# A hybrid encoder layer: keys and first queries summed while the normalised input comes in quarters, attention ahead of the late rows' queries, and a gate in column tiles

## The chip, the cores and the metric

The kernel runs on one core of a Trainium2 chip. The metric is the device time of one execution in microseconds (us), as the median of several runs. The core has five engines with an instruction queue each: TensorE (PE), VectorE (DVE), ScalarE (ACT), GpSimd (POOL) and SyncE (SP). Each engine executes its queue in order and waits on semaphores for the others. All transfers of this kernel are issued by SP.

## What is computed

One encoder layer is applied to two groups of 1024 rows of 1024 numbers ("prompt" and "sample"), which share the weights and have a conditioning vector c each. In short, for one group:

```python
mod = silu(c) @ w_ada + b_ada
shift, scale, gate = split(mod, 3)
h = rms_norm(x, norm_g) * (1 + scale) + shift
qa, ka, va, za, qb, kb, vb, zb, ga, gb = split(h @ w_in)     # 5376 columns in all
# branch A: 8 query heads, 2 key and value heads, 64 wide
oa = attention(rope(norm(qa)), rope(norm(ka)), va) * silu(za)
# branch B: 4 heads with two softmax maps each, values 128 wide
pd = softmax(q0 k0) - lam * softmax(q1 k1)
ob = rms_norm(pd @ vb, subln_g) * (1 - lam_init) * silu(zb)
merged = sigmoid(ga) * (oa @ w_proj_a) + sigmoid(gb) * (ob @ w_proj_b)
y = x + gate * (merged @ w_out)
```

## The kernel before

The numbers are 32-bit floats. Most products are made from a rounded high part and a remainder of each operand (`h` has parts `hh` and `hl`, a weight `w` has two parts in one tile): three matmuls for each block of 128 inputs, hh x w-high, hh x w-low and hl x w-high. ACT makes the high part by a copy, DVE the remainder by a subtraction.

The transposed input lies as eight blocks of 128 channels by 1024 rows, in two halves of 512 rows. Every piece of work is a generator that yields after each portion of TensorE work, and `weave` (line 71) interleaves generators by how far each has come relative to its planned number of portions; tables of numbers at the top (lines 37 to 60) set these plans for each group and phase. A scheduler then orders the instructions on each engine, so the order on an engine is not simply that of the code.

- `start` (line 337) loads w_ada's parts for shift and scale (eight tiles of 512 x 512), the first half of x, the weight for keys and values, and the second half of x. `ada` (line 292) multiplies c with w_ada, TensorE giving two output rows of 512 columns at a time (line 298). `inv_rms` and `spread` make 1/rms of each row from squares (line 254), and `modulated` makes h's parts for the first half of the rows, `start_late` for the second.
- `kva_gen` and `qa_gen` sum keys with values, and queries, tile by tile of 128 rows (`proj_tt`, line 515: 24 matmuls with 256 columns). A front part normalises and rotates on ACT, DVE and POOL, a back part transposes (line 568). Before attention starts, the head has summed eight tiles of keys and eight of the first queries.
- `z_gen` sums a gate path: four units a call of 24 matmuls with 512 columns (line 704), 48 units in a group. They are the filler: `Z_HEAD` and `Z_SHARE` say how many run in which phase.
- `attention` (line 872) makes for each tile of 128 queries four score matmuls (lines 737 and 738; the second takes a copy of the queries with halves swapped by a transfer), a maximum on DVE (739), an exponential on ACT (741), a transpose on DVE (774) and a transfer that completes it, then the products with the values (799 and 800 in branch A, 839 in branch B). There are 64 score tiles in branch A and 64 in branch B in a group; they are counted through here, 0 to 127 for the first group and 128 to 255 for the second.
- At the end of attention `gate_gen` multiplies c with the gate's third of w_ada (line 452, 16 matmuls, first group alone), and `gated_gen` multiplies the outputs by their gates; for branch B it puts 1/rms of each row into 128 equal rows by four transposes for each block and half (line 942). `merge_gen` (976) and `out_gen` (1007) do the last products; `TAIL` portions of branch A's merge are kept until attention is over.

PSUM has two large tiles for scores ("s"), three of one bank ("f") and one for values ("a"). Outside attention the "f" requests may take an "s" tile (`gbank`, line 120).

## Time and profile before

| | us |
|---|---|
| median of 3 runs | 1944.24 |
| lowest and highest run | 1936.62, 1945.65 |
| profiled execution | 1933.24 |
| its span, first to last instruction | 1931.5 |
| TensorE busy | 1881.2 |
| DVE busy | 1397.3 |
| ACT busy | 991.7 |
| POOL busy | 414.7 |

The profile is of one execution. A row of a group names the line of the kernel, the engine, the operation, output and input tiles without their numbers, shapes and count; then the busy time of the group, the mean duration of one instruction in ns, and how long the engine had idled before them with what ended most of that. A matmul of full 32-bit floats (line 298, for example) appears as two passes. A row of a stretch of time has the busy time of PE, PE's weight loads, DVE, ACT and POOL, each with its number of instructions, then the clock that TensorE was granted (1.00 is full speed), the busy share of the transfer engines and GB/s. Matmuls overlap, so the mean duration of one is longer than what it adds to the busy time.

### The profile page before, as it was taken

To read this page: it belongs to the slowest core of one execution; us is meant where nothing else is said; L and a number is where in the kernel's file an instruction comes from. 1 tells how busy PE (TensorE), PEld (TensorE's weight loads), DVE (VectorE), ACT (ScalarE), POOL (GpSimd) and SP (SyncE) were. 2 spreads that over 40 slices of the span, in tenths; PEclk is the share of its full clock that TensorE was granted. 3 is DMA by queue.
4 is the path that set the end of the run, shared out by engine and by line. 5 is a ranking of instruction groups with operands and counts; after the bars stand their busy time and mean duration, and the time that the engine had idled before them with its cause. 6 is when DMAs were issued, how large, how long until landed. Compare 5 with 4: busy or idle time off the path is not lost.

```text
span 1931.5 us, 30797 instructions
## 1 busy us (share of the span) xinstructions
PE 1881.2 (97%) x10466; PEld 1610.0 (83%) x10466; DVE 1397.3 (72%) x2145; ACT 991.7 (51%) x2091; POOL 414.7 (21%) x758
## 2 busy tenths in 40 slices
...
GB/s 319 45 81 146 135 173 148 153 148 176 152 142 110 116 92 192 273 256 181 218 140 39 137 144 166 145 172 151 154 129 162 107 113 100 143 234 264 180 104 77
DMA packets 271613, 295.25 MB, mean 153 GB/s; under 512 B 37857, under 2 KB 220257, under 8 KB 271457
## 3 DMA queue, kind: packets, MB, share of 16 engines
...
## 4 chain that ended last, share of the span: by engine, by line
PE 81%; DVE 7%; DMA 5%; issue 2%; ACT 2%; SPq 1%; POOL 1%; DVEq 0%; ACTq 0%; POOLq 0%
PE f L704 22%; PE f L515 19%; PE f L1007 5%; PE s L737 5%; PE a L839 5%; PE s L738 5%; PE f L976 4%; PE s L1007 4%; PE a L800 3%; PE a L799 3%; PE s L976 2%; DMA q<-p 2%; DVE m L739 2%; DVE p L774 1%; PE f L298 1%
## 5 line engine op out<-in xcount | busy, mean ns | idle before, releaser
L704 PE MATMUL f<-u,w 128*128 128x512 f32 x2232 | 574.2, 395 | 2.0 <-DVE ssB L863 1.5
L515 PE MATMUL f<-w,u 128*128 128x256 f32 x3456 | 487.5, 285 | 7.5 <-DVE u L571 3.7
L515 PEld LDWEIGHTS f<-w,u 128*128 128x128 f32 x3456 | 457.8, 190 | 29.0 <-DVE u L571 4.3
L704 PEld LDWEIGHTS f<-u,w 128*128 128x128 f32 x2232 | 404.2, 188 | 77.8 <-DVE ssB L863 1.8
L739 DVE TENSOR_REDUCE m<-s 128x1 f32<-128x1024 f32 x256 | 311.0, 1217 | 51.3 <-PE s L738 48.4
L774 DVE STREAM_TRANSPOSE p<-p 128x1024 f32<-128x1024 f32 x192 | 238.3, 1241 | 92.7 <-ACT p L741 89.3
L738 PE MATMUL s<-u,sw 128*128 128x512 f32 x512 | 203.8, 398 | 0.0
L788 DVE TENSOR_TENSOR q<-q,hi 128x512 fp32r<-128x512 f32 x256 | 171.5, 690 | 34.3 <-ACT hi L787 32.3
L787 ACT ACTIVATE hi<-q 128x512 fp32r<-128x512 f32 x256 | 153.6, 624 | 76.2 <-DMA q<-p 37.8
L741 ACT ACTIVATE p<-s,m,rsA 128x1024 f32<-128x1024 f32 x128 | 153.8, 1202 | 71.4 <-DMA q<-p 69.6
L178 ACT ACTIVATE w<-st 128x512 fp32r<-128x512 f32 x196 | 114.4, 625 | 99.2 <-DMA st<-in_w_in_dram 42.4
L741 ACT ACTIVATE p<-s,m,rsB 128x1024 f32<-128x1024 f32 x128 | 154.3, 1205 | 6.5 <-DMA q<-p 1.9
L179 DVE TENSOR_TENSOR w<-st,w 128x512 fp32r<-128x512 f32 x196 | 132.8, 706 | 34.2 <-ACT w L178 33.1
L658 POOL TENSOR_TENSOR row<-row,gB 128x96 f32<-128x96 f32 x64 | 33.8, 528 | 485.7 <-ACT row L529 474.1
L799 PE MATMUL a<-hi,u 128*128 128x256 f32 x512 | 132.2, 284 | 2.8 <-DMA q<-p 1.8
L800 PE MATMUL a<-q,u 128*128 128x256 f32 x512 | 129.3, 286 | 2.6 <-DVE q L788 2.6
L976 PE MATMUL f<-u,w 128*128 128x512 f32 x540 | 130.5, 393 | 1.3 <-DVE u L987 1.3
L839 PE MATMUL a<-q,u 128*128 128x256 f32 x512 | 127.1, 385 | 3.9 <-DVE oo L816 3.0
L976 PEld LDWEIGHTS f<-u,w 128*128 128x128 f32 x540 | 100.5, 188 | 23.0 <-DVE u L987 2.3
L839 PEld LDWEIGHTS a<-q,u 128*128 128x128 f32 x512 | 95.6, 193 | 20.0 <-DVE oo L816 3.6
L737 PE MATMUL s<-u 128*128 128x512 f32 x256 | 108.3, 424 | 3.3 <-ACT p L741 3.2
L737 PE MATMUL s<-u,u 128*128 128x512 f32 x256 | 102.4, 400 | 8.5 <-ACT p L741 3.1
(181 smaller groups left out, 2557.5 us busy)
## 6 DMA issues: line engine op xcount, KB each, us to landing
...
sw<-u SPq DMA_DIRECT2D x256, 64.0 KB, 2.1
...
```

Of the source, the lines that this page charges most:

```text
L515: nc.tensor.matmul(ps, lt[c][:, sl], w[:, c, wi, :], start=(k == 0), stop=(k == 23))
L704: nc.tensor.matmul(ps, w[:, c, wi, e * P : (e + 1) * P], rt[c], start=(k == 0), stop=(k == 23),)
L737: nc.tensor.matmul(s[:, sl], q, k[:, sl], start=True, stop=False)
L738: nc.tensor.matmul(s[:, sl], sw, k[:, sl], start=False, stop=True)
L739: nc.vector.tensor_reduce(out=m, in_=s, axis=AX.X, op=ALU.max, negate=True)
L741: nc.scalar.activation(pt.rearrange("p (j c a) -> p j c a", j=4, c=8), s.rearrange("p (c a j) -> p j c a", c=8, j=4), AF.Exp, scale=rs, bi ...
L774: nc.vector.transpose(pt, pt)
L799: nc.tensor.matmul(acc, lt, th[:, c, :], start=(k == 0), stop=False)
L800: nc.tensor.matmul(acc, lt, tl[:, c, :], start=False, stop=(k == 7))
L839: nc.tensor.matmul(acc, u["v"][:, k], pT[:, k], start=(k == 0), stop=(k == 7))
L976: nc.tensor.matmul(ps, w[:, c, wi, d * P : (d + 1) * P], o[:, oi, :], start=(k == 0), stop=(k == 11))
L1007: nc.tensor.matmul(ps, w[:, c, wi, e * P : (e + 1) * P], m[:, mi, :], start=(k == 0), stop=(k == 23))
```

## The change

- The start: w_ada comes as four quarters of 256 channels, each with shift and scale, and x's first half ahead of them all on SP's queue. The weight for the first 256 query columns is loaded at the start too, and a gate weight after x's second half. `ada` holds c in 32 columns (two used, the rest zero) and places four matmuls on four groups of 32 columns of the array (`tile_position`); four small matmuls with `two` then add the four groups (`ada_sum`). After each quarter, two blocks of h are made and their matmuls for keys with values (tile s_251) and for queries (s_252) of the first four row tiles are done at once (`sums_early`), the eight sums standing in the two "s" tiles. `in_order` keeps these instructions in the order of the code among themselves.
- The late half's squares are added on DVE ahead of their matmuls (line 271 had 36 matmuls in all, there are 8 now).
- The head: the key tiles 4 to 7 are summed as before, the four early query tiles get their front and back part, and attention starts; the other four query tiles run beside it.
- Filler: the tables of numbers are new (two of them are in the diff); the first group has about 46.7 gate-path units ahead of its last phase instead of 43, the second 41 instead of 40.
- The gate: four times eight matmuls of 256 columns in column tiles, after the gate paths instead of ahead of them.
- Branch B's 1/rms: one transpose for two heads, a copy, a transfer to DRAM and from there a transfer to 128 partitions for each block and half.

```diff
...
 Z_SHARE = (
-    (7, 19, 6, 3, 2, 4),
-    (9, 14, 7, 3, 2, 6),
+    (8, 19, 6, 3, 3, 3),
+    (13, 12, 7, 3, 0, 6),
...
-TAIL = 5
-TAIL_A = 0.3
...
+TAIL = (2, 5)
+TAIL_A = (1.15, 1.15)
...
+class in_order:
+    def __init__(self, tc, engine):
+        self.tc, self.engine = tc, engine
+    def __getattr__(self, name):
+        op = getattr(self.engine, name)
+        return lambda *a, **k: self.tc.keep_in_program_order(op(*a, **k))
...
-        if alone[0] and turn[0] % 5 in (0, 2):
+        if alone[0] and not early and turn[0] % 5 in (0, 2):
...
-        hf, third, q = n // 4, n // 2 % 2, n % 2
+        quarter, q = n // 2, n % 2
         wt = chunks4(utile().bitcast(F32))
-        row, col = q * 512, third * D + hf * 512
-        dma(wt, w_ada[row : row + 512, col : col + 512].rearrange("(c p) n -> p c n", p=P))
+        for third in range(2):
+            row, col = q * 512, third * D + quarter * 256
+            dma_next(
+                wt[:, :, third * 256 : third * 256 + 256],
+                w_ada[row : row + 512, col : col + 256].rearrange("(c p) n -> p c n", p=P),
+            )
         return wt
...
+    def ada(wts, cpad):
+        acc = gbank()
+        for q, wt in enumerate(wts):
+            for c in range(4):
+                pe.matmul(
+                    acc[32 * c : 32 * c + 32], cpad[:, q * 4 + c], wt[:, c], start=(q == 0), stop=(q == 1),
+                    tile_position=(0, 32 * c),
+                )
+        part = rtile()
+        act.activation(part, acc, AF.Copy)
+        return part
+    def ada_sum(part):
+        ps = gbank()[:, :8].rearrange("p (t c g) -> p t c g", t=2, g=2)
+        for third in range(2):
+            for c in range(2):
+                o = third * 256 + c * P
+                pe.matmul(ps[:, third, c], part[:, o : o + P], two, start=True, stop=True)
+        return ps
...
     def modulated(ht, hf, xT, cs):
         for c in cs:
             scale, shift = modc[:, 1, c, 0:1], modc[:, 0, c, 0:1]
...
+            hh, hl = (x[c] for x in ht[hf][:2])
+            act.activation(hh, xT[c], AF.Identity, scale=scale, bias=shift)
+            vec.tensor_scalar(
+                out=xT[c], in0=xT[c], scalar1=scale, scalar2=shift, op0=ALU.mult, op1=ALU.add
+            )
+            vec.tensor_tensor(out=hl, in0=xT[c], in1=hh.bitcast(F32), op=ALU.subtract)
...
+    def sums_early(ht, c, n):
+        hh, hl = (x[c] for x in ht[0][:2])
+        w = kva_w[n][0]
+        for tt in (1, 0, 3, 2) if c == NCH - 1 else range(4):
+            sl = slice(tt * P, (tt + 1) * P)
+            for k, (lt, wi) in enumerate(((hh, 0), (hh, 1), (hl, 0))):
+                first, last = c == 0 and k == 0, c == NCH - 1 and k == 2
+                pe.matmul(
+                    early[n][tt], lt[:, sl], w[c][:, wi, :],
+                    start=(first and tt % 2 == 0), stop=(last and tt % 2 == 0),
+                )
+    def four_sums():
+        s = sbank()
+        return [s[:, i * 256 : i * 256 + 256] for i in range(4)]
...
+        xT = [load_xT0(0)]
+        dma_next(bcol, t["b_col"])
+        dma_next(gcol, t["g_col"])
         wts = [load_ada(n) for n in range(2)]
...
+        kva_w.append(load_w(w_cols(w_in, (C_KA, 256)), early=True))
+        kva_w.append(load_w(w_cols(w_in, (C_QA, 256)), early=True))
+        wts += [load_ada(n) for n in range(2, 8)]
+        rs = inv_rms(added(squares(xT[0])))
         nc.vector.tensor_scalar(out=bcol[:, 1, :], in0=bcol[:, 1, :], scalar1=1.0, scalar2=None, op0=ALU.add)
...
+        rsb = spread(rs)
+        early.update({n: four_sums() for n in range(2)})
+        ps = ada_sum(ada(wts[:2], cpad))
+        with tc.high_priority(offset=QUARTER_P):
+            for quarter in range(4):
+                cs = range(quarter * 2, quarter * 2 + 2)
+                by_rms(xT[0], cs, rsb)
+                split_early(kva_w[0][1], quarter)
+                ada_end(quarter, ps)
+                if quarter % 2 == 0:
+                    add_h(ht, 0, quarter // 2)
+                split_early(kva_w[1][1], quarter, act)
+                modulated(ht, 0, xT[0], cs)
+                split_early(kva_w[1][1], quarter, vec)
+                for c in cs:
+                    sums_early(ht, c, 0)
+                part = ada(wts[quarter * 2 + 2 : quarter * 2 + 4], cpad) if quarter < 3 else None
+                for c in cs:
+                    sums_early(ht, c, 1)
+                    if part is not None:
+                        ps, part = ada_sum(part), None
         xT.append(load_xT0(1))
...
+        kva_w.append((load_w(w_cols(w_in, (C_ZA, 256)), room=(utile(), utile())),))
+        return lambda: inv_rms(added(squares(xT[1]))), lambda rs: start_late(ht, xT[1], rs)
...
+            x, hh = xT[c], ht[1][0][c]
+            vec.scalar_tensor_tensor(out=x, in0=x, scalar=modc[:, 1, c, 0:1], in1=rsb, op0=ALU.mult, op1=ALU.mult)
+            act.activation(hh, x, AF.Identity, bias=modc[:, 0, c, 0:1])
+            act.activation(x, x, AF.Identity, bias=modc[:, 0, c, 0:1])
+            for d in {0: (), 7: (6, 7)}.get(c, (c - 1,)):
+                vec.tensor_tensor(out=ht[1][1][d], in0=xT[d], in1=ht[1][0][d].bitcast(F32), op=ALU.subtract)
+            if c % 2:
+                yield 1
...
+        for n in range(4):
+            acc = gbank()[:, :256]
+            nc.vector.memset(acc, 0.0)
+            for q in range(2):
+                sts = []
+                for i in range(2):
+                    st = spool.tile([P, 2, 256], F32, tag="st", name=nm("st"))
+                    row, col = q * 512 + i * 256, 2 * D + n * 256
+                    dma(st, w_ada[row : row + 256, col : col + 256].rearrange("(c p) n -> p c n", p=P))
+                    sts.append(st)
+                for c in (2, 3, 0, 1):
+                    nc.tensor.matmul(
+                        acc[32 * c : 32 * c + 2], cT[:, q * 4 + c], sts[c // 2][:, c % 2], start=(q == 0), stop=(q == 1),
+                        tile_position=(0, 32 * c),
+                    )
+                yield 1
+            part = rtile()[:, :256]
+            nc.vector.tensor_copy(part, acc)
+            ps = gbank()[:, :4].rearrange("p (c g) -> p c g", g=2)
+            for c in range(2):
+                nc.tensor.matmul(ps[:, c, :], part[:, c * P : (c + 1) * P], two, start=True, stop=True)
...
+    def proj_tt(ht, w, tt, given={}):
+        if tt in given:
+            for _ in CUTS:
+                yield 1
+            return given[tt]
...
+            if tt + 1 == rest:
+                while pend:
+                    back(*pend.pop(0))
...
+                        while not units[n][2]() and next(feed, None) is not None:
+                            pass
...
+        if i > 1 and hf == 0:
+            ss = st["ssB"][:, 2 * i - 4 : 2 * i - 2].rearrange("p j n -> p (j n)")
+            ps = fbank()[:16, :P]
+            nc.tensor.transpose(ps, ss, ident)
+            row = rtile()[:16, :P]
+            nc.scalar.activation(row, ps, AF.Copy)
+            dma(st["rB"][i - 2], row)
...
-                rb = gbank()
-                for k in range(4):
-                    r = st["ssB"][:, e - 4, hf * 4 + k : hf * 4 + k + 1]
-                    nc.tensor.transpose(rb[:, k * P : (k + 1) * P], r.to_broadcast([P, P]), ident)
+                dma(rb, rB[e % 2, hf].partition_broadcast(P))
...
-            for i in range(2):
-                weave((islice(kva, 6), 6, 0.0), (islice(zs, 3), 3, 0.0))
-                if i == 0:
-                    late()
-            weave((chain(kva, qa), 40, 0.0), (islice(zs, nz - 6), nz - 6, Z_HEAD_A[g]))
+            rs = late[0]()
+            weave((islice(zs, 6), 6, 0.0), (late[1](rs), 4, LATE_A))
+            weave((kva, 27, 0.0), (islice(zs, Z_FIRST[0]), Z_FIRST[0], Z_FIRST_A[0]))
+            drain(islice(qa, KV_STEPS))
+            early.clear()
+            folded()
         else:
-            weave((chain(kva, qa), 52, 0.0), (islice(zs, nz), nz, Z_HEAD_A[g]))
+            weave((kva, 27, 0.0), (islice(zs, Z_SPLIT), Z_SPLIT, Z_HEAD_A[0]))
+            folded()
+            weave((qa, 27, 0.0), (islice(zs, nz - Z_SPLIT), nz - Z_SPLIT, Z_HEAD_A[1]))
+        return qa
...
+        if g == 0:
+            weave((islice(att, FIRST_ATT), FIRST_ATT, 0.0), (qa, 15, FIRST_A), (islice(zs, Z_FIRST[1]), Z_FIRST[1], Z_FIRST_A[1]))
...
+            yield from zs
             if g == 0:
                 yield from gate_gen()
-            yield from zs
             drain(first)
-            yield from islice(merge, 16 - TAIL)
+            yield from islice(merge, 16 - TAIL[g])
...
-        weave((until_next(att), LAST_ATT, 0.0), (fill(), LAST_FILL, 0.0), (gates(), 12, GATED_A))
+        weave((until_next(att), LAST_ATT[g], 0.0), (fill(), LAST_FILL[g], 0.0), (gates(), 12, GATED_A[g]))
...
```

TensorE's queue at the very start. u_164 and u_166 are the first two tiles of w_ada before, u_181 and u_184 those of its first quarter now; q is x's squares, ps and rs the 1/rms. Before:

```order
L298 MATMUL f_202<-u_164,cT 2x512 x4
L298 MATMUL f_202<-u_166,cT 2x512 x4
L307 MATMUL f_218<-ident,p_216 128x2 x4
L298 MATMUL s_211<-u_177,cT 2x512 x4
L271 MATMUL f_242<-ones_c,q_228 128x1 x4
L298 MATMUL s_211<-u_179,cT 2x512 x4
L298 MATMUL f_267<-u_181,cT 2x512 x4
L285 MATMUL s_252<-ident,rs_248 128x128 x4
```

The same queue now (line 105 is that of `in_order`, which issues all operations that go through it):

```order
L308 MATMUL f_233<-ones_c,q_219 128x1 x4
L322 MATMUL s_244<-ident,rs_239 128x128 x4
L105 MATMUL f_253<-u_181,at_167 32x512 x4
L105 MATMUL f_253<-u_184,at_167 32x512 x4
L105 MATMUL f_264<-two,row_262 128x2 x4
L105 MATMUL s_251<-w_187,u_275 128x256 x2
L105 MATMUL s_251<-w_187,u_276 128x256
```

The sums of squares and the spread of 1/rms moved ahead of the modulation, and sums of keys follow the first quarter at once.

ACT's queue between the third and the fourth quarter: q_600 and q_601 are squares of the late half (before q_347 and q_348), w_187 and w_194 the key and the query weight, u_575 the gate weight, u_433 the high parts of h's blocks 4 to 7. Before:

```order
L321 ACTIVATE u_171<-u_171,modc 128x512 x2
L326 ACTIVATE u_289<-u_171 128x512 x4
L254 ACTIVATE q_347<-u_196 128x512 x4
L254 ACTIVATE q_348<-u_197 128x512 x4
L321 ACTIVATE u_172<-u_172,modc 128x512 x2
L326 ACTIVATE u_333<-u_172 128x512 x4
```

Now:

```order
L105 ACTIVATE u_433<-u_174,modc 128x512 x2
L292 ACTIVATE q_600<-u_569 128x512 x4
L105 ACTIVATE row_476<-f_467 128x512
L105 ACTIVATE w_187<-p_191 128x2x256
L105 ACTIVATE w_194<-p_198 128x2x256
L292 ACTIVATE q_601<-u_570 128x512 x4
L203 ACTIVATE u_575<-st_577 128x2x256
L105 ACTIVATE u_433<-u_174,modc 128x512 x2
```

The late squares stand ahead of the second half of h in both; now two weight splits and a gate weight's split stand there as well, and sums of keys and queries wait behind them.

DVE's queue over score tiles 117 to 119 of the first group (m are the maxima, p the exponentials, row and tab belong to `gated_gen`). Before:

```order
L739 TENSOR_REDUCE m_8343<-s_8344 128x1
L456 COPY row_8323<-f_8250 2x512
L739 TENSOR_REDUCE m_8378<-s_8379 128x1
L461 TENSOR_TENSOR gatec<-f_8325,bcol 128x8
L760 RECIPROCAL r_8352<-su_8342 128x1
L464 TENSOR_SCALAR gatec<-gatec 128x8
L773 SCALAR_TENSOR_TENSOR p_8305<-p_8341,r_8352,p_8305 128x1024
L739 TENSOR_REDUCE m_8400<-s_8401 128x1
```

Now:

```order
L826 TENSOR_REDUCE m_8647<-s_8648 128x1
L1041 TENSOR_TENSOR row_8450<-tab_8454,row_8450 128x512
L847 RECIPROCAL r_8586<-su_8576 128x1
L860 SCALAR_TENSOR_TENSOR p_8552<-p_8575,r_8586,p_8552 128x1024
L1034 TENSOR_TENSOR row_8495<-row_8495,row_8496 128x512
L826 TENSOR_REDUCE m_8691<-s_8692 128x1
L1043 TENSOR_TENSOR u_8449<-row_8450,u_8449 128x512
L861 STREAM_TRANSPOSE p_8552<-p_8552 128x1024
L1041 TENSOR_TENSOR row_8495<-tab_8499,row_8495 128x512
L847 RECIPROCAL r_8700<-su_8690 128x1
```

The steps of `gated_gen` stand between the maxima where few were before, and the gate's come later.

253 lines of the change are left out of this document (112 added, 141 removed).

## The prediction

> **What bounds the kernel now.** I read the page's busy times first, then the busy time by stretches of 10 and 25 us, then TensorE's groups up to the first attention score, and last the stretches in which TensorE waits. Busy times, from the page:
>
> ```profile
> span 1931.5 us, 30797 instructions
> PE 1881.2 (97%) x10466; PEld 1610.0 (83%) x10466; DVE 1397.3 (72%) x2145; ACT 991.7 (51%) x2091; POOL 414.7 (21%) x758
> L704 PE MATMUL f<-u,w 128*128 128x512 f32 x2232 | 574.2, 395 | 2.0 <-DVE ssB L863 1.5
> ```
>
> TensorE (PE) is busy for all but 50.3 us. So an edit counts only by TensorE work that it removes or by TensorE waits that it fills or opens. A 512-column matmul costs TensorE 574.2/2232 = 0.257 us. Next, TensorE's first instruction and the first score from the timeline, and its groups up to that score (columns at the end: busy us, mean ns of one, idle before):
>
> ```profile
> 6.85 9.21 PE L298 MATMUL f<-u,cT 128*2 128x512 f32 x16 [6.85 <-DMA u<-in_w_ada_dram]
> 138.57 0.50 PE L737 MATMUL s<-u,u 128*128 128x512 f32 x1 [2.84 <-DVE ev L712]
> L515 PE MATMUL f<-w,u 128*128 128x256 f32 x384 | 50.6, 285 | 3.3 <-DVE ev L712 3.1
> L298 PE MATMUL f<-u,cT 128*2 128x512 f32 x48 | 23.3, 642 | 6.8 <-DMA u<-in_w_ada_dram 6.8
> L704 PE MATMUL f<-u,w 128*128 128x512 f32 x72 | 18.2, 395 | 0.0
> L704 PE MATMUL s<-u,w 128*128 128x512 f32 x48 | 14.0, 437 | 0.0
> L271 PE MATMUL f<-ones_c,q 128*128 128x1 f32 x72 | 10.2, 271 | 0.0
> L298 PE MATMUL s<-u,cT 128*2 128x512 f32 x16 | 7.2, 592 | 0.0
> L568 PE MATMUL f<-ident,row 128*128 128x128 f32 x12 | 2.7, 281 | 2.8 <-DVE row L557 1.8 <-POOL row L557 1.0
> ```
>
> The work that must be done in any order is 384 sums of 256 columns (0.132 each, 50.6), 120 gate-path matmuls (30.8) and 22 transposes (0.225 each, 5.0): 86.4 us. The first score comes at 138.6, so the start is 52.2 us behind. 30.5 of that is modulation (64 passes of 0.476), 10.2 the sums of squares.
>
> **The change part by part. First, the start.** Transfers set its pace; the stretches of 10 us (after the five engines: granted clock, DMA share, GB/s), and the durations of the chain:
>
> ```profile
> 0.00:10.00 10.00, 3.15 (x4) 0.50 (x5) 0.65 (x5) 1.50 (x2) 0.69 (x6) 1.00 0.81 267
> 10.00:20.00 10.00, 9.14 (x24) 1.93 (x23) 4.99 (x6) 4.59 (x8) 0.00 (x0) 1.00 1.05 406
> 20.00:30.00 10.00, 10.00 (x35) 3.06 (x34) 3.58 (x8) 3.12 (x5) 1.22 (x2) 1.00 1.06 402
> 30.00:40.00 10.00, 10.00 (x24) 1.87 (x22) 9.78 (x14) 6.31 (x11) 3.45 (x2) 1.00 1.06 362
> L254 ACT ACTIVATE q<-u 128x512 f32<-128x512 f32 x16 | 8.8, 616 | 8.6 <-DMA u<-in_xT_prompt_dram 8.4
> L321 ACT ACTIVATE u<-u,modc 128x512 f32<-128x512 f32 x4 | 3.2, 812 | 4.0 <-POOL u L356 1.9 <-DVE u L356 1.4 <-DVE modc L315 0.7
> L327 DVE TENSOR_TENSOR u<-u,u 128x512 fp32r<-128x512 f32 x8 | 5.0, 679 | 1.1 <-ACT u L326 1.1
> L533 POOL TENSOR_TENSOR rsA<-ss,nhalf 128x4 f32<-128x4 f32 x4 | 4.1, 1015 | 5.5 <-DVE ss L532 5.5
> ```
>
> By these rates, in the new order on SP's queue, x is in at 9.5 us, the first quarter of w_ada at 13.7, both weights at 18.9, the other quarters at 24.1, 29.4 and 35.1, the tables at 36.5, the late x at 43. That 1 KB lines replace 2 KB lines is taken as free: the weights have such lines now, inside the 402 GB/s stretch.
>
> The first quarter: squares end at 11.9 (four of 0.616 after the second half), additions at 13.9, sums, powers (1.015) and the spread at 17.1. Then eight modulation matmuls in two sets of four column tiles. No row shows column tiles. If the four of a set run at once, a quarter's two sets take four passes, 1.9 us; if one after the other, 16 x 0.476 = 7.6. I take 1.9, since each writes other partitions, and keep 7.6. Copy 0.6, four small sums 1.0, two short DVE steps 0.35, ACT 0.81: the early sums begin at 21.9. A quarter then holds TensorE for 48 x 0.132 + 1.9 + 1.0 = 9.2 us, longer than its transfer (5.2), ACT's work (3.5) or DVE's (5.4: eight of about 0.68). Three quarters end at 49.5.
>
> The fourth waits. By the order ACT squares the second half of the late x (4 x 0.616) and splits a gate weight ahead of the fourth quarter's h, and DVE does three additions and a split ahead of its remainders. I make that 4.3 us, then 6.3 of sums, 1.0 for the late sum of squares, 0.65 for its spread: 61.8. Then 30.8 of gate path, 12.7 of late keys, 3.2 of transposes: 108.5. At the end the last key tile goes through POOL behind query tiles (3.2 us of waiting), a weight is split late (1.0), query transposes wait 0.8, and the scores wait 4.5 for the swapped queries' transfer: with two half scores 118.5. A cold TensorE clock costs some 2.5 (below): 121.0. The work then left undone against before is four query tiles, 96 x 0.132, and eight transposes, less what has begun: 13.9 us. So 121.0 stands against 138.6 - 13.9 = 124.7: **-3.7**, from -17.5 (no such waits) to +19 (serial tiles, 4 x 5.7 more). SP's new rows ahead of these (tables, gate weight) add nothing else: TensorE is behind the transfers by then.
>
> **Two rows that a rule bears on.** Stretches of 4 us at group 1's passage from branch A to branch B, and some 65 us on:
>
> ```profile
> 1416.00:1420.00 4.00, 1.92 (x10) 1.29 (x9) 4.00 (x7) 3.15 (x7) 1.57 (x2) 1.00 0.58 169
> 1420.00:1424.00 4.00, 1.45 (x4) 0.67 (x4) 3.91 (x6) 2.77 (x8) 2.56 (x6) 0.62 0.76 200
> 1424.00:1428.00 4.00, 3.79 (x14) 3.41 (x15) 3.14 (x4) 2.68 (x8) 0.00 (x0) 0.52 0.45 117
> 1428.00:1432.00 4.00, 1.95 (x12) 1.46 (x10) 3.97 (x7) 3.22 (x8) 0.00 (x0) 1.00 0.26 63
> 1480.00:1484.00 4.00, 1.22 (x6) 0.60 (x4) 3.91 (x5) 1.94 (x5) 0.00 (x0) 0.80 0.44 142
> 1484.00:1488.00 4.00, 3.23 (x8) 2.61 (x9) 3.36 (x5) 2.26 (x5) 0.34 (x1) 0.50 0.61 151
> 1488.00:1492.00 4.00, 4.00 (x17) 3.33 (x16) 0.80 (x3) 0.39 (x1) 0.00 (x0) 0.84 0.53 137
> ```
>
> After waits of some 2 to 3 us the granted clock is about 0.5 for 4 to 6 us; 3.79 busy at 0.52 lose 1.8 us. That is where my 2.5 for the start comes from, where TensorE waits longer. The Trainium skill, "TensorE: Matmul & The Clock Gate", Part 1, says that about 3.4 us of idleness halve the clock until about 3.4 us of work; the rows agree in size. The skill's "TensorEngine Tiling (Array Packing)", sections Key Properties and Theoretical Speedup, says that tiles run in parallel, up to four times faster, but that each change of tiling drains TensorE, which speaks against this change; no run here shows either. With an estimated drain of 395 - 257 = 0.14 us at some 22 changes the sum would be 3 us higher.
>
> **The gate, the 1/rms of branch B, the moved fill.** Rows of TensorE over the whole run, 25 us stretches at the ends of attention, and DVE's and a b-value row:
>
> ```profile
> L452 PE MATMUL f<-st,cT 128*2 128x512 f32 x32 | 15.2, 592 | 1.2 <-DMA st<-in_w_ada_dram 1.2
> L459 PE MATMUL f<-ident,row 2*128 2x2 f32 x8 | 0.8, 203 | 0.2 <-DVE row L456 0.2
> L861 PE MATMUL f<-ones_c,at 128*128 128x1 f32 x128 | 16.0, 229 | 0.0
> L942 PE MATMUL f<-ident,ssB 128*128 128x128 f32 x60 | 8.9, 273 | 0.8 <-DVE u L987 0.8
> L942 PE MATMUL s<-ident,ssB 128*128 128x128 f32 x4 | 0.6, 272 | 0.0
> L839 PE MATMUL a<-q,u 128*128 128x256 f32 x512 | 127.1, 385 | 3.9 <-DVE oo L816 3.0 <-issue 0.3 <-DMA q<-p 0.2
> 750.00:775.00 25.00, 23.13 (x85) 12.46 (x84) 21.08 (x30) 12.19 (x24) 3.19 (x6) 1.00 0.74 223
> 775.00:800.00 25.00, 23.03 (x105) 19.04 (x104) 18.22 (x27) 11.81 (x23) 0.69 (x2) 1.00 0.81 249
> 800.00:825.00 25.00, 23.46 (x107) 18.88 (x106) 18.77 (x29) 9.04 (x17) 1.10 (x3) 1.00 0.94 316
> 1650.00:1675.00 25.00, 23.01 (x124) 19.66 (x122) 22.04 (x37) 15.51 (x35) 8.77 (x19) 1.00 0.56 159
> L739 DVE TENSOR_REDUCE m<-s 128x1 f32<-128x1024 f32 x256 | 311.0, 1217 | 51.3 <-PE s L738 48.4
> L774 DVE STREAM_TRANSPOSE p<-p 128x1024 f32<-128x1024 f32 x192 | 238.3, 1241 | 92.7 <-ACT p L741 89.3
> ```
>
> 1/rms: 64 transposes (9.5) go, four stay (0.6): **-8.9**, for the merges behind them keep TensorE busy. The way through DRAM, some 10 us of copy, two transfers and three steps, is hidden behind the merge matmuls that the order puts after each L1014; if not, the gain falls to 0. Its 16 reads of 0.26 MB are 4.2 MB, 10 us of transfer at 400 GB/s, in stretches that are up to 0.94 full.
>
> Gate: 15.2 and 0.8 (L459) go; 64 half-length passes four at a time (3.8) and 16 small ones of 0.125 (2.0) come: -10.2. But the fill that stood in group 0's last phase (3.7 units of 24 x 0.257, 23 us) has moved to earlier phases. Counting the order's rows over the last eleven score tiles, TensorE has 11 x 1.03 of scores, 24 b-values of two 0.248 passes, the gate and little else, 30.3 us; DVE has 42.7 (eleven maxima of 1.217, six each of transposes and pair sums of about 1.25, sixteen row steps of 0.68, small ones). TensorE waits 12; before it waited 1.9 + 2.0 + 1.5 = 5.4. Together -10.2 + 6.6 = **-3.6** (-10.2 to +2); serial tiles would cost nothing here, being inside the wait.
>
> Group 1, A to B: at the second wait (score tiles 200 to 204) the order's rows gave TensorE 11.2 us of work against DVE's 11.2; now 18.1 against 13.2. So it goes: 2.8 + 0.8 idle and 2.5 lost to the clock, **-6.0**. At the first the balance stays (12.2 against 16.1; before 14.8 against 19.0); I leave it, with -9 as the far end. Group 1, end of attention: tiles 236 to 240 now have 10.2 of TensorE against 19.8 of DVE (before 19.5 against 24.3, and 2.0 waited): I take 7 waited, **+5.0** (0 to +8).
>
> **Sum.** -3.7 - 8.9 - 3.6 - 6.0 + 5.0 = -17.2. The profiled execution took 1933.24 (span 1931.5 and 1.7 around it): 1916.0. The runs' median, 1944.24, stands 0.57% above it (runs 1936.62 to 1945.65), and I expect the same of the change: 1927, 0.9% faster.
>
> **Rivals.**
> The start's waits are covered: at 43 to 50 us ACT has slack and could have squared earlier, were transfers a little faster. The 13.8 us go, and the time is 1902, or 1913 by the median.
> Both ends of attention cost more: DVE also waits there for ACT and POOL, as its idle 89.3 at L774 shows. With 8 more at the first and 4 at the second: 1928, or 1939, within 0.5%, which is about what a measurement tells from no change.
> The column tiles do not run together, and the time is slower: four quarters' matmuls at 7.6, or 9.2 as the row at 6.85 shows for the first 16 passes, add 22.8 to 29: 1939 to 1945, by the median 1950 to 1956. It decides above 6.2 us a quarter, where the sum is zero. For it: they share one stream of instructions and 128 rows each; against: they share no columns. The skill's page on the clock gate, Part 3, gives 2.38 times for three such tiles; an estimate from it is near my sum.
> The change does not do what it says: the order places all but nine of the 192 early sums ahead of the first gate-path matmul, so this can only fail in time, as above.
>
> **How the numbers follow.** As forecast 0.42; start covered 0.22; ends dearer 0.16; serial 0.13; something unseen, slower, 0.07. Faster by over 0.5%: 0.42 + 0.22 less the forecast's edge near 1934.5, 0.62. Within: 0.18, the dearer ends and that edge. Slower: 0.20. The range goes from a covered start in a fast run, 1899, to the serial case, 1951; the forecast's own is 1915 to 1938.
>
> **What would show it.** Early sums from 22 us; a quarter's eight 32x512 matmuls in 1.9 us; a wait of about 4 us near 50; first scores near 121 us; TensorE waiting some 12 us on DVE over group 0's last tiles and 7 in group 1's; the dip at 1480 gone; no wait on the 1/rms reads. Eights of 7 us, scores after 125 us or waits over 20 us at an end would make the forecast wrong.

## The result, and the profile after

The changed kernel takes 1958.77 us (median of five runs, 1953.03 to 1961.24) against 1943.93 for the kernel before (five runs, 1936.62 to 1945.65): a ratio of 1.0086, 95% interval 1.0069 to 1.0102. It is 0.9% slower, where 0.9% faster was forecast, and outside the range. The two profiled executions took 1953.03 and 1933.24 us, 19.8 apart.

From the page of the changed kernel, span and busy times, and from TensorE's groups the largest of those with the gate path's matmuls (L704 before; over all groups there are 2304 of them in both kernels):

```profile
span 1951.2 us, 30752 instructions
PE 1865.0 (96%) x10406; PEld 1609.4 (82%) x10406; DVE 1398.9 (72%) x2160; ACT 994.9 (51%) x2095; POOL 412.1 (21%) x766
L797 PE MATMUL f<-u,w 128*128 128x512 f32 x2136 | 547.1, 394 | 4.5 <-DVE w L204 2.3 <-ACT w L203 1.1 <-ACT row L1009 0.6
```

TensorE is 16.2 us less busy (1881.2 before), and waits 86.2 us instead of 50.3. So work did go, and more than that came back as waits. Where it did is read from the busy times in seven stretches, cut at the same events in both kernels: group 0's first score, the first score matmul of the last 16 of its 128 score tiles ("the last eighth"), its first output matmul (`out_gen`), and the same three of group 1. The kernel before (columns: length, then busy time of PE, PEld, DVE, ACT, POOL, then granted clock, DMA share, GB/s):

```profile
0.00:138.60 138.60, 121.47 (x687) 89.53 (x687) 82.82 (x209) 61.52 (x144) 41.79 (x68) 0.98 0.45 151
138.60:727.90 589.30, 583.77 (x3490) 518.65 (x3491) 468.16 (x655) 368.71 (x777) 152.43 (x291) 1.00 0.51 140
727.90:910.10 182.20, 176.13 (x770) 133.03 (x769) 132.61 (x199) 64.06 (x120) 11.09 (x23) 1.00 0.71 227
910.10:1074.50 164.40, 164.40 (x922) 144.05 (x921) 95.20 (x205) 59.03 (x141) 46.06 (x66) 1.00 0.42 140
1074.50:1667.10 592.60, 575.83 (x3431) 510.38 (x3429) 468.63 (x659) 366.83 (x778) 152.01 (x295) 0.99 0.51 138
1667.10:1840.50 173.40, 172.36 (x789) 142.48 (x788) 128.09 (x190) 63.91 (x121) 11.34 (x17) 1.00 0.66 211
```

And the changed kernel:

```profile
0.00:124.30 124.30, 89.80 (x541) 72.97 (x541) 73.21 (x179) 53.74 (x120) 24.19 (x50) 0.92 0.52 161
124.30:754.70 630.40, 619.16 (x3670) 547.75 (x3670) 483.21 (x693) 380.15 (x807) 172.96 (x322) 0.99 0.52 135
754.70:934.30 179.60, 158.54 (x709) 123.06 (x708) 131.16 (x206) 63.86 (x119) 9.96 (x18) 0.91 0.76 234
934.30:1101.40 167.10, 167.10 (x933) 146.18 (x932) 93.18 (x200) 56.12 (x136) 43.48 (x62) 1.00 0.40 136
1101.40:1689.40 588.00, 575.40 (x3432) 510.19 (x3430) 466.22 (x659) 369.37 (x780) 147.27 (x292) 0.99 0.54 141
1689.40:1860.20 170.80, 167.79 (x746) 137.34 (x746) 130.12 (x195) 63.98 (x123) 14.24 (x24) 0.99 0.72 224
```

The seventh, 91.0 us of output, is the same in both. A busy TensorE at half clock does half the work, so I split each length into idle time, lost clock (busy time times one minus the granted clock, summed over stretches of 2 us) and what is left, the work:

| stretch | before: length = work + idle + lost clock | after |
|---|---|---|
| 1, start to first score | 138.6 = 118.5 + 16.7 + 3.4 | 124.3 = 83.2 + 34.6 + 6.4 |
| 2, to the last eighth | 589.3 = 583.4 + 5.9 + 0 | 630.4 = 615.1 + 11.1 + 4.2 |
| 3, to the first output matmul | 182.2 = 176.1 + 6.1 + 0 | 179.6 = 146.3 + 21.1 + 12.2 |
| 4, to group 1's first score | 164.4 = 164.4 + 0 + 0 | 167.1 = 167.1 + 0 + 0 |
| 5, to its last eighth | 592.6 = 571.2 + 16.8 + 4.6 | 588.0 = 571.6 + 12.6 + 3.8 |
| 6, to its first output matmul | 173.4 = 172.4 + 1.0 + 0 | 170.8 = 166.7 + 3.0 + 1.1 |

Work falls by 35.9 us over the whole, idle time and lost clock rise by 55.6. The third row has the surprise: TensorE has 29.8 us less to do there, and the stretch is only 2.6 us shorter. Most of the work missing in it was not removed: 72 gate-path matmuls, 18.5 us, stand in stretch 2 instead, which also has the four late query tiles and is 41.1 us longer.

What stretch 3 looks like from TensorE, five rows of the changed kernel's timeline with their waits (start, us, then in brackets the idle time before and its releaser):

```profile
784.22 0.79 PE L824 MATMUL s<-u 128*128 128x512 f32 x1 [3.87 <-ACT p L828]
799.95 1.03 PE L528 MATMUL f<-st,cT 128*2 128x256 f32 x8 [4.62 <-DMA st<-in_w_ada_dram]
818.45 1.03 PE L528 MATMUL f<-st,cT 128*2 128x256 f32 x8 [3.56 <-DMA st<-in_w_ada_dram]
827.44 1.03 PE L528 MATMUL f<-st,cT 128*2 128x256 f32 x8 [2.57 <-DMA st<-in_w_ada_dram]
838.05 0.66 PE L537 MATMUL f<-two,row 128*128 128x2 f32 x4 [2.92 <-DVE row L534]
```

The gate's sets of four wait for their loads, and the scores for the softmax. Around and after each such wait the granted clock is 0.5, for 3.4 to 10.2 us at a time.

The start, in the same view:

```profile
16.95 3.05 PE L105 MATMUL f<-u,at 128*32 128x512 f32 x16
23.09 0.79 PE L105 MATMUL s<-w,u 128*128 128x256 f32 x2 [1.31 <-ACT u L105]
29.39 1.95 PE L105 MATMUL f<-u,at 128*32 128x512 f32 x16
122.13 0.66 PE L649 MATMUL f<-ident,row 128*128 128x128 f32 x2 [4.95 <-DVE row L638]
124.25 0.79 PE L824 MATMUL s<-u,u 128*128 128x512 f32 x1
```

Sixteen column-tile passes take 1.95 us (the first sixteen took 3.05, at a granted clock that the trace gives as 1.00; why is not shown), the early sums begin at 23.1, and the first score comes at 124.25. So the start went nearly as forecast. A wait that the forecast does not have, 4.95 us before the last query transposes, came from DVE, which stood in order on branch B's tables; their transfers were issued at 108 to 114 us, behind a late weight on SP's queue. The start has a tail in stretch 2:

```profile
124.30:132.00 7.70, 5.67 (x16) 3.75 (x16) 7.04 (x17) 1.82 (x5) 4.71 (x7) 0.51 0.07 18
```

TensorE is idle for 2.0 us there and the clock is half, which loses some 2.8 more: 4.8 us of the 15.3 that stretch 2 loses.

### The profile page after: what moved, and what is told of

It is laid out like the page before. It is cut to its first block, busy times and chain, and to the rows that moved or that the text cites. A ratio compares the mean times of both kernels' runs of the same rounds, so it can differ in the third digit from the quotient of the medians.

```text
span 1951.2 us, 30752 instructions
## 1 busy us (share of the span) xinstructions
PE 1865.0 (96%) x10406; PEld 1609.4 (82%) x10406; DVE 1398.9 (72%) x2160; ACT 994.9 (51%) x2095; POOL 412.1 (21%) x766
## 4 chain that ended last, share of the span: by engine, by line
PE 58%; DVE 14%; DMA 11%; SPq 7%; issue 4%; ACT 4%; POOL 2%; ACTq 0%; DVEq 0%; POOLq 0%
PE f L596 13%; PE f L797 12%; PE f L1070 6%; DMA q<-p 6%; PE f L1101 6%; SPq L866 5%; PE a L926 4%; PE s L1101 3%; PE s L824 3%; PE s L825 3%; DVE m L826 3%; DVE q L875 3%; DVE p L861 2%; PE s L1070 2%; ACT p L828 1%
## 5 line engine op out<-in xcount | busy, mean ns | idle before, releaser
L797 PE MATMUL f<-u,w 128*128 128x512 f32 x2136 | 547.1, 394 | 4.5 <-DVE w L204 2.3
L596 PE MATMUL f<-w,u 128*128 128x256 f32 x3264 | 456.0, 285 | 0.7 <-DVE u L652 0.5
L797 PEld LDWEIGHTS f<-u,w 128*128 128x128 f32 x2136 | 387.8, 188 | 79.7 <-DVE w L204 3.5
L596 PEld LDWEIGHTS f<-w,u 128*128 128x128 f32 x3264 | 428.9, 191 | 18.2 <-DVE u L652 0.9
L828 ACT ACTIVATE p<-s,m,rsB 128x1024 f32<-128x1024 f32 x128 | 154.4, 1206 | 14.8 <-DMA q<-p 7.2
L203 ACT ACTIVATE w<-st 128x512 fp32r<-128x512 f32 x188 | 109.3, 625 | 99.2 <-PE f L1101 34.3
L204 DVE TENSOR_TENSOR w<-st,w 128x512 fp32r<-128x512 f32 x188 | 126.3, 703 | 32.9 <-ACT w L203 32.2
L1070 PE MATMUL f<-u,w 128*128 128x512 f32 x576 | 140.0, 395 | 0.6 <-DVE u L1043 0.5
L1070 PEld LDWEIGHTS f<-u,w 128*128 128x128 f32 x576 | 108.7, 190 | 24.8 <-DVE u L1043 0.9
L825 PEld LDWEIGHTS s<-u,sw 128*128 128x128 f32 x512 | 99.5, 194 | 17.6 <-issue 1.1
```

The source lines that it names most:

```text
L596: nc.tensor.matmul(ps, lt[c][:, sl], w[c][:, wi, :], start=(k == 0), stop=(k == 23))
L797: nc.tensor.matmul(ps, w[c][:, wi, e * P : (e + 1) * P], rt[c], start=(k == 0), stop=(k == 23),)
L825: nc.tensor.matmul(s[:, sl], sw, k[:, sl], start=False, stop=True)
L828: nc.scalar.activation(pt.rearrange("p (j c a) -> p j c a", j=4, c=8), s.rearrange("p (c a j) -> p j c a", c=8, j=4), AF.Exp, scale=rs, bi ...
L1070: nc.tensor.matmul(ps, w[:, c, wi, d * P : (d + 1) * P], o[:, oi, :], start=(k == 0), stop=(k == 11))
```

## The experiments

My theories were three at first: that the gate's loads through three buffers make the waits of stretch 3, that the fill moved out of it makes them, and that late tables cost the start 5 us. Times are given as ratios to the kernel before, run beside each; the changed kernel's own is 1.0086. "Lost" is idle time and lost clock together, from the profiled execution.

**The tables early.** The nine transfers moved ahead on SP's queue, right behind branch A's tables:

```
     load_tables()
+    lamw = fetch_tables_B()
     for g in range(2):
...
-            load_tables_B()
+            load_tables_B(lamw)
```

> The changed kernel, with branch B's tables, weights and lambda vectors (the nine transfers that follow the first late weight on SP's queue at 108 to 114 us) issued right behind the tables of branch A, at about 45 us. Theory, that these transfers hold up DVE at 113.5 to 121 us and with it the last query transposes (the 4.95 us wait of L649): the wait goes, the first score comes 4 to 5 us earlier (119.5 to 120.5 us instead of 124.25), and the time falls by 4 to 5 us from 1958.8, to about 1954. Rival, that the swapped queries' transfer or the query tiles' own steps on DVE and POOL are as late anyway: the first score moves by less than 1.5 us and the time by less than 2.

Ratio 1.0096 (1.0080 to 1.0113); first score at 124.59. The wait of 4.95 us shrank to 0.68, but up to the first score TensorE lost 40.9 us, as in the changed kernel (41.0): waits of 1.14 and 0.79 us opened at 85 and 87 us, and more clock went. By the first score the rival held. But the run does not clear the tables: DVE now waits for them earlier, 4.00 us up to 66.6 and 2.96 up to 70.8, and starts the late rows' steps at 72.2 us instead of 68.6. The stall was moved and not removed, so what the start would gain without it is not shown.

**The gate's loads in buffers of their own**, and then **the gate at two other places**: ahead of the units that are left (its old place), and between the merge matmuls of branch B.

```
-                    st = spool.tile([P, 2, 256], F32, tag="st", name=nm("st"))
+                if q == 0:
+                    wt = utile().bitcast(F32).rearrange("p (c n) -> p c n", c=8)
```

> The changed kernel, with the gate's weights read into the large u buffers, one of 128x8x256 for each quarter, instead of passing 16 pieces through the three st buffers; the column tiles and their place stay. Theory one, that the loads through three buffers make the waits at group 0's end of attention (waits of L528 on st: 4.6, 3.6, 2.6, 1.2 us, 11.9 in all, and a clock of 0.77 to 0.81 behind them): waits in 775 to 850 us fall from 20 to under 10 us, and the time falls by 10 to 15 us, to 1944 to 1949. Theory two, that the work moved out of the last phase makes them: the waits are then put down to DVE or ACT instead, and the time falls by less than 4 us.

```
         def fill():
-            yield from zs
             if g == 0:
                 yield from gate_gen()
+            yield from zs
```

> The changed kernel, with the gate (column tiles) at its old place, ahead of the units still left for the last phase instead of behind them. If the order of gate and units is what costs, the waits on st fall below 4 us and the time by 8 to 12 us. If it is the amount of work left, or the loads, it moves by less than 4 us.

```
-        weave((merge_gen(st, 1, oT, mT), 8, 0.0), (then[1][1], 4, 1.0))
+        weave((merge_gen(st, 1, oT, mT), 8, 0.0), (then[1][1], 4, 1.0), (gate_gen() if g == 0 else iter(()), 4, 0.0))
```

> The changed kernel, with the gate (its column tiles as they are) taken out of the last phase of attention of group 0 and put between the merge matmuls of branch B, where TensorE has nothing to wait for; the branch-A merges take its place beside the last scores. Theory, that the gate's place is what costs (its set of four waits for loads that pass three buffers, and it is the only filler there): idle time in 760 to 870 us falls from 20 to under 8, and the time by 15 to 20 us, to 1939 to 1944. Rival, that the last score tiles are bounded by the softmax steps on DVE and ACT whatever stands between: the waits are put down to ACT at the scores and the time falls by less than 5 us.

The last of the three also changes a pace number of the last phase, `LAST_FILL`, from 21 to 15, since the gate's portions are gone from it. Ratios 1.0122 (1.0105 to 1.0139), 1.0102 (1.0085 to 1.0120) and 1.0147 (1.0125 to 1.0169): none is faster than the changed kernel. Stretch 3 with the gate in own buffers, and with the gate in the merges:

```profile
756.50:939.60 183.10, 159.73 (x708) 122.49 (x707) 130.44 (x206) 60.53 (x116) 12.43 (x22) 0.93 0.75 226
```

```profile
759.30:941.60 182.30, 155.02 (x705) 119.78 (x703) 125.78 (x197) 56.83 (x110) 12.23 (x22) 0.94 0.73 218
```

It lasts 183.1 and 182.3 us, with 33 us lost in both, as in the changed kernel (33.3); with the gate ahead of the units it is 185.0, with 38 lost. With own buffers the waits for the gate's weights fell from 11.9 to 6.3 us, and waits for the exponentials (6.9) and for stored probabilities read back (5.3) took their place. In the merges, the waits went to the merges themselves (10 us idle from 870 to 940). So neither other buffers nor another place for the gate shortened the stretch.

**Without the gate's computation.**

```
     def gate_gen():
-        for n in range(4):
...
+        nc.vector.memset(gatec, 0.5)
+        yield 1
```

> The changed kernel without the gate's computation (constants in its place): 16 loads, 64 and 16 matmuls left out. If the gate's loads and waits set the stretch, it falls from 179.5 to 160 to 168 us (11.9 and 3.5 us of waits and their clock, 5.8 us of work). If not, the waits pass to the scores and it falls by less than 6 us.

```profile
754.80:924.40 169.60, 148.69 (x629) 119.71 (x628) 127.20 (x189) 59.30 (x113) 13.83 (x22) 0.93 0.73 218
```

(`LAST_FILL` is 15 here too.) Stretch 3 falls by 9.9 us, between the two expectations; some 6 of that is the gate's work, so about 4 us of its waits were its own, and 29 us are still lost. The whole time did not move (1.0091, 1.0061 to 1.0120), for group 1, with the same code, took 939.5 us instead of 925.9 between the two first output matmuls.

**Fill put back into the last phase**: first the units alone, then the whole last phase of group 0 as before, then that with all of group 0's old numbers, so that only the start and the 1/rms are left of the change there.

```
-    (8, 19, 6, 3, 3, 3),
+    (7, 18, 5, 3, 2, 5),
...
-LAST_FILL = (21, 25)
+LAST_FILL = (30, 25)
```

> The changed kernel, with 4 units more of 24 matmuls each (24.7 us of TensorE) kept for the last phase of group 0, taken from the earlier phases of attention: shares 7, 18, 5, 3, 2 instead of 8, 19, 6, 3, 3. Gate, its place and its loads stay. Theory two, that the moved work makes the waits at group 0's end: they fall from 20 us to under 8 and the time by 8 to 14 us, to 1945 to 1951, less what the earlier phases lose. Theory one, that the loads make them: the L528 waits on st stay at 8 us or more in all and the time moves by less than 4 us.

```
-LAST_ATT = (47, 45)
-LAST_FILL = (21, 25)
-GATED_A = (0.1, 0.1)
-TAIL = (2, 5)
+LAST_ATT = (44, 45)
+LAST_FILL = (26, 25)
+GATED_A = (-0.3, 0.1)
+TAIL = (5, 5)
...
-                nc.tensor.matmul(ps[:, c, :], part[:, c * P : (c + 1) * P], two, start=True, stop=True)
+                nc.tensor.transpose(ps[:, c, :], row[:, c * P : (c + 1) * P], ident[:2, :2])
```

> The changed kernel with the last phase of group 0 as before: full-width gate matmuls, gate ahead of the remaining units, 5 units left for it (shares 7, 18, 5, 3, 2), and the old weights of that phase. If group 0's end of attention lost what the two traces say (20 us of waits and some 4 us of clock against 5.4 us, less 10 us of gate work), the time falls by 8 to 14 us, to 1945 to 1951: about the kernel before. If the loss lies in the earlier phases or in group 1, it falls by less than 4 us.

The third has that last phase and gate too, and besides:

```
-    (8, 19, 6, 3, 3, 3),
+    (5, 19, 6, 3, 2, 5),
...
-    (0.944, 1.018, 1.232, 1.187, 1.03, 1.769),
+    (1.07, 0.933, 1.1, 0.95, 1.129, 1.52),
```

> The changed kernel with group 0's attention as before: the old weights and leads of its phases, 5.3 units left for the last phase (shares 5, 19, 6, 3, 2, since 1.7 units more are done ahead), full-width gate in its old place, old pace numbers. What is left of the change in group 0 is the start and the 1/rms through DRAM. Theory, that moved fill made the loss: TensorE's idle time and lost clock between 230 and 870 us fall from 43 us towards 10, and the time falls by 12 to 20 us, to 1939 to 1947. Rival, that the early first scores themselves leave attention short of cover (the query tiles that come after them): the loss stays above 30 us and the time above 1953.

Ratios 1.0251 (1.0233 to 1.0268), 1.0216 (1.0198 to 1.0234) and 1.0172 (1.0150 to 1.0193): all slower than the changed kernel. Stretches 2 and 3 of the last one:

```profile
124.60:757.60 633.00, 609.55 (x3594) 538.74 (x3594) 480.84 (x689) 376.64 (x802) 165.93 (x316) 0.98 0.51 132
757.60:945.70 188.10, 178.32 (x745) 133.14 (x745) 132.11 (x201) 67.04 (x128) 12.11 (x23) 0.98 0.75 235
```

Stretch 3 is nearly full again: 12.8 us lost, and 175.3 of work. But stretch 2 now loses 35.2 us (15.3 in the changed kernel, 5.9 before), most of it before 420 us. The sum over both is 48.0, against 48.6 and 12.0; over the 230 to 870 us of the expectation it is 34.5, against 43.1 and 10.1. By the number written down the rival holds, and the loss before 420 us fits it: once the first scores come early and four query tiles come after them, the old numbers leave the first phases of attention short. What set of numbers would not was not looked for. So fill put back does not mend the changed kernel; what its move cost is read from the kernel before, next.

**Single parts in the kernel before.** The moved fill alone, the column tiles alone at the gate's old place, and the 1/rms through DRAM alone:

```
-    (7, 19, 6, 3, 2, 4),
+    (8, 21, 7, 3, 2, 1),
...
-LAST_FILL = 26
+LAST_FILL = 19
```

> The kernel before, with four units of group 0's last phase (96 matmuls, 24.7 us) moved to the earlier phases, alone: shares 8, 21, 7, 3, 2 instead of 7, 19, 6, 3, 2. Theory, that the last stretch is not TensorE's to shorten: the earlier part grows by 20 to 25 us, the stretch to the first output matmul shrinks by under 12, TensorE's waits there rise to 12 us or more, and the time rises by 10 to 18 us, to 1950 to 1958. Forecast's reckoning (moved work costs only the waits that open, some 6 us): 1942 to 1949.

```
-                nc.tensor.matmul(acc, cT[:, k], st, start=(k == 0), stop=(k == NCH - 1))
+                    nc.tensor.matmul(
+                        acc[32 * c : 32 * c + 2], cT[:, q * 4 + c], sts[c // 2][:, c % 2], start=(q == 0), stop=(q == 1),
+                        tile_position=(0, 32 * c),
+                    )
```

> The kernel before, with the gate by column tiles alone, at the gate's old place. TensorE's gate work falls from 16.0 us to between 5.8 (my sum) and 9.5 (measured in the changed kernel, partly at a low clock). Theory, that tiles are cheap where other work stands beside them: 5 to 9 us faster, 1935 to 1939. Rival, that the tiles' loads of 16 pieces through three buffers stall TensorE here too, since a set of four takes two pieces at once: no faster, or up to 8 us slower.

```
-                rb = gbank()
-                for k in range(4):
...
+                dma(rb, rB[e % 2, hf].partition_broadcast(P))
```

> The kernel before, with branch B's 1/rms through DRAM alone (64 transposes of 9.5 us for four and 16 reads). By my forecast 8.3 to 8.9 us faster, 1935 to 1936. Rival, that the reads or the row's way through DRAM hold up the gated products: the gain falls to under 3 us.

Ratios 1.0156 (1.0135 to 1.0177), 1.0143 (1.0124 to 1.0161), 1.0039 (1.0025 to 1.0052). Each part alone makes the kernel before slower as a whole (the controls below say how much of that can be the order alone). Stretches 2 and 3 with the fill moved, then stretch 3 with the column tiles, then with the 1/rms:

```profile
141.10:759.00 617.90, 609.13 (x3587) 538.67 (x3588) 467.64 (x659) 372.60 (x785) 148.09 (x291) 0.99 0.50 137
759.00:935.90 176.90, 157.50 (x674) 117.94 (x673) 129.73 (x195) 60.10 (x112) 11.69 (x23) 0.96 0.70 222
```

```profile
732.70:923.10 190.40, 173.82 (x810) 137.61 (x809) 133.34 (x209) 66.20 (x124) 14.37 (x23) 0.96 0.72 221
```

```profile
733.70:919.10 185.40, 175.16 (x740) 131.66 (x739) 132.38 (x200) 66.47 (x126) 11.95 (x23) 0.98 0.75 238
```

With the fill moved, 22.2 us of work leave stretch 3 and it becomes 5.3 shorter; stretch 2 grows by 28.6. That is the changed kernel's pattern (2.6 shorter, 41.1 longer) from this part alone. With the column tiles 9.1 us of work go and 17.3 more are lost; with the 1/rms 3.5 go and 6.7 more are lost. Wherever TensorE gives up work in this stretch, waits take its place.

**What sets the stretch.** Up to the first merge matmul the stretch takes 84.6 us before and 83.9 after, though TensorE's work in it falls from 80 to some 53 us (first row before, second after):

```profile
728.00:812.60 84.60, 80.11 (x331) 54.08 (x330) 62.37 (x88) 37.97 (x76) 7.40 (x18) 1.00 0.75 229
```

```profile
754.70:838.60 83.90, 63.58 (x296) 45.80 (x294) 64.11 (x95) 34.05 (x68) 6.08 (x13) 0.84 0.79 233
```

The last eleven score tiles up to the same matmul, the piece that the prediction balanced, again before and after:

```profile
750.70:812.60 61.90, 58.06 (x245) 41.93 (x245) 47.30 (x68) 29.25 (x57) 3.87 (x8) 1.00 0.80 250
779.20:838.60 59.40, 39.08 (x178) 25.76 (x174) 46.52 (x69) 22.39 (x44) 3.78 (x8) 0.77 0.85 255
```

DVE does the same 62 to 64 us of steps up to the first merge matmul. Its waits there in the changed kernel (columns: us in total, times, longest):

```profile
DVE r L847 <- ACT p L828: 6.1, 4, 2.4
DVE row L1034 <- DMA row<-zd: 5.5, 6, 1.8
DVE m L826 <- PE s L825: 2.5, 4, 1.0
DVE row L1037 <- DMA row<-zd: 2.0, 1, 2.0
DVE p L860 <- POOL r L848: 1.3, 4, 0.5
DVE row L1041 <- DMA tab<-rA: 1.0, 1, 1.0
```

Busy time and waits of an engine that works in order add up to the length of any stretch (62.4 and 21.9 us before, as well), so their sum does not tell which engine holds it up. For whom DVE waits tells more: 2.5 us for TensorE's scores, 8.5 for reads of the gated products, 6.1 for exponentials (before: 2.2, 8.9 and 2.8). And SP, which issues all transfers in order, stands in the way too. The end of the chain that leads to the wait of 4.62 us shown above (start, us, what):

```profile
793.48 0.58 DVE row L1041
794.14 0.60 SPq L866
794.79 0.60 SPq L866
795.44 0.91 SPq L866
796.39 3.52 DMA st<-in_w_ada_dram
799.95 1.03 PE f L528 x8
```

A step of the gated products on DVE ends, SP issues the transfers that complete a transposed tile, and only then the gate's next load. I tried to shorten DVE's line, first by leaving out the products with z and the reads of z, in the changed kernel and in the kernel before:

```
-            dma(z, st["zd"][(e, hf)])
...
-                nc.vector.tensor_tensor(out=o, in0=o, in1=z, op=ALU.mult)
+                nc.vector.tensor_tensor(out=o, in0=rb, in1=o, op=ALU.mult)
```

> The changed kernel without the product of each head's output with z in the gated products (both groups): 16 DVE steps of 0.69 us and 16 reads of z a group are left out, no TensorE work. From the last eighth of group 0's score tiles to its first output matmul the changed kernel takes 179.6 us with TensorE busy 158.5 of them; before it was 182.2 with 176.1. Theory, that this stretch of the changed kernel is set by DVE's steps and the reads they wait for (DVE 131 us busy, waits of 7.5 us on z in 70 us), not by TensorE: it shrinks by 8 to 15 us, and the whole time falls by 10 to 22 us. Rival, that TensorE's own waits on the gate's loads set it: it shrinks by less than 4 us.

> The kernel before without the same products with z. By the theory that TensorE is the bound of this stretch there (176.1 busy of 182.2), it shrinks by less than 5 us, and the time by 0 to 8 us: clearly less than in the changed kernel. If DVE bounds both alike, both fall alike.

Ratios 1.0117 (1.0102 to 1.0132) and 0.9958 (0.9942 to 0.9973). The kernel before moved as written, its stretch 3 from 182.2 to 180.7 us; the changed kernel, which should have gained more, gained nothing. Its stretch 3 stayed at 181.0 us; DVE's steps to the first merge fell to 58.0 us in 81.0, and it waited longer for scores (6.3). Then by leaving out the arithmetic of all gated products, with the reads of z and of the spread rows:

```
             dma(o, st["od"][e][hf])
-            dma(z, st["zd"][(e, hf)])
-            rb = mtile("tab", [P, 512])
...
-            nc.vector.tensor_tensor(out=o, in0=rb, in1=o, op=ALU.mult)
             nc.scalar.activation(u[:, c, 0, :], o, AF.Copy)
```

> The changed kernel without the gated products' arithmetic in both groups: a head's output is read and split as it is; the products with z and 1/sum or 1/rms, and the reads of z and of the spread rows (some 20 us of DVE, 32 and more reads a group), are left out. TensorE's work is the same. Theory one, that DVE's line in this stretch (64.9 us busy and 18.8 us of waits in 85) sets its length: from the last eighth to the first output matmul 179.5 us become 160 to 170. Theory two, that the round of a score tile through maximum, exponential and its two buffers sets it, whatever DVE does beside: 174 to 180.

```profile
758.20:927.20 169.00, 157.65 (x709) 122.14 (x708) 111.59 (x174) 63.10 (x119) 9.52 (x18) 0.94 0.66 196
```

Now stretch 3 is 169.0 us, 10.5 shorter with the same work on TensorE, and 20.7 us are lost instead of 33.3; the whole time is 1.0016 (1.0003 to 1.0029). This is inside the range of theory one, and clear of the variants above that keep these products, the gate and the amount of fill, whose stretch 3 takes 179.2 to 185.0 us. So the gated products hold up the stretch. By which of their parts is not separated: the edit takes out DVE's steps, but also the reads that DVE waits for, their share of the transfers, and their places in SP's queue (85 transfers up to the first merge instead of 116, at some 0.5 us of SP each). The 20.7 us that stay are not explained by it.

**Controls.** The order of instructions is planned from a simulated timeline, so an edit ahead of group 1 also changes the order inside group 1, whose code is the same. To see what that alone costs, one pace number of the last phase was changed by one, in the kernel before and in the changed one:

```
-LAST_FILL = 26
+LAST_FILL = 25
```

> The kernel before with one pace number of group 0's last phase changed from 26 to 25: the same instructions, in an order that differs in 56 blocks of DVE's rows, 27 of them in group 1. Theory, that the kernel before sits on an order that its numbers were chosen for, and any other order costs some us: 3 to 12 us slower. Rival, that the order's small differences are worth nothing: within 2 us.

```
-LAST_FILL = (21, 25)
+LAST_FILL = (22, 25)
```

> The changed kernel with the same pace number changed from 21 to 22. Theory as for the kernel before: 2 to 10 us slower. Rival: within 2 us.

Ratios 1.0002 (0.9989 to 1.0014) and 1.0125 (1.0104 to 1.0146). The kernel before does not mind; the changed kernel loses 0.39%, some 7.6 us. So a difference under 8 us between two variants of the changed kernel says nothing of the edit's purpose, and this is one edit only: another order can cost more. From first output matmul to first output matmul, group 1 takes 930.4 us before, 934.4 in the control, and with the same group-1 code 937.8 with the fill moved and 946.1 with the column tiles: of the column tiles' loss, 15.7 us are there, by the other order alone.

**The 1/rms by transposes again**, in the changed kernel, and **group 1's numbers alone**, in the kernel before:

```
-                dma(rb, rB[e % 2, hf].partition_broadcast(P))
+                rb = gbank()
+                for k in range(4):
...
```

> The changed kernel with branch B's 1/rms spread by 64 transposes again. If the row through DRAM gains there what the stretches from first merge to first output say (1.8 and 4.0 us against before): 4 to 8 us slower, 1963 to 1967. If the transposes only filled waits, as in the kernel before: within 3 us.

```
-    (9, 14, 7, 3, 2, 6),
+    (13, 12, 7, 3, 0, 6),
...
-    (1.15, 1.354, 1.035, 1.196, 0.85, 1.069),
+    (1.017, 1.209, 1.063, 1.196, 0.764, 1.069),
```

> The kernel before with the changed kernel's numbers for group 1 alone (shares, weights and leads of its phases; the last phase's own numbers stay). By the traces the waits and lost clock of 1200 to 1600 us were 20 us before and 10 us after, and the end of group 1 lost 4 more: 4 to 8 us faster, 1932 to 1936, which would beat both kernels. Rival, that the numbers only suit the order that the changed kernel has up to there: no gain, within 4 us of before.

Ratios 1.0148 (1.0127 to 1.0168) and 1.0008 (0.9995 to 1.0021). The first is some 12 us slower than the changed kernel, more than the control, but not by enough to show a gain of the 1/rms: its stretch 6 is 178.3 us instead of 170.8, and in the control, with the same code there, it is 176.2. The second gains nothing: stretch 5 is 5.0 us shorter, the other two of group 1 together 7.2 longer. None of the kernels that compute the whole reference beats the kernel before.

## Why the prediction was wrong

The forecast's sum was -17.2 us on the profiled execution; measured is +19.8. Term by term, by the table of stretches:

| term of the sum | forecast | measured |
|---|---|---|
| start, against the work that it leaves undone | -3.7 | -0.5 |
| waits in the rest of group 0's attention (stretch 2) | none taken | +9.4 |
| waits and lost clock at group 0's end (stretch 3) | +6.6 | +27.2 |
| group 1, A to B (stretch 5) | -6.0 | -5.0 |
| group 1, end (stretch 6) | +5.0 | +3.1 |
| gate and 1/rms, work of TensorE | -19.1 | -14.4, as what remains of the 19.8 |

Counted from TensorE's groups, the last term is 14.8: the gate falls from 16.0 to 9.5 us (-6.5, where -10.2 was forecast; part of it ran at half clock), the 1/rms from 9.5 to 1.2 (-8.3, where -8.9 was forecast).

**Start: right in its steps, 3 us late.** Early sums at 23.1 (21.9 said), two sets of tiles in 1.95 us (1.9), the wait of the fourth quarter there (3.7 us between 52 and 64 us; 4.3 said), the first score at 124.25 (121.0), just under the limit of 125. By the forecast's break-even of 124.7 the start is worth 0.5 us, and the 4.8 us lost right behind the first score take more than that. The rival of serial tiles is out.

**Group 0's end: the step that failed.** It was "TensorE waits 12; before it waited 1.9 + 2.0 + 1.5 = 5.4. Together -10.2 + 6.6". TensorE was idle for 21.1 us in stretch 3, over the 20 that the prediction named as its limit. Its two sums for the last eleven score tiles were nearly right: 30.3 us of TensorE work (28.6 measured) and 42.7 of DVE steps (46.5). Three things are wrong in the step. It took DVE's steps as the time that the tiles need, but they took 59.4 us, and 61.9 before, when TensorE's work in them was twice as much: a second engine's busy time is the least that a stretch can take, not its length. It priced idle time and not the clock after it: 12.2 us, though the prediction quotes rows with a clock of 0.5 and charges 2.5 us for them at the start and in group 1. And it took moved fill as free except for the wait. The run with the fill moved alone shows that the fill's old place cost little: 22.2 us of work left it for 5.3 us of time, and stretch 2 grew by 28.6. The last phase was long for other reasons, the gated products among them, and TensorE's work in it was almost free. The rival "both ends of attention cost more" came nearest, with 8 us more at the first end; it was 20.6. It named DVE's waits for ACT and POOL; of 18.8 us of DVE's waits these were 7.8, and 8.5 were reads.

**1/rms: right in work, wrong in cover for the kernel before.** Alone in the kernel before it cost 0.39%: in stretches 3 and 6 it took away 7.5 us of TensorE's work, and 13.2 more were lost there. That the transposes had filled waits for the gated products fits this but is not shown by itself. The prediction's far end for this term, a gain of 0, was not far enough there; in the changed kernel no run separates its worth from that of the order.

**Group 1: right in both terms, by their sizes.** 5.0 of 6.0 and 3.1 of 5.0. The second wait that the forecast named is gone (at score tiles 200 to 204 one of 0.9 us is left, at full clock), but the 5.0 is a balance of several waits, and the numbers that do it gained nothing in the kernel before.

**Left open.** Why stretch 2 loses 9.4 us more (4.8 us are lost right behind the first score), and 29 more where the old numbers are put back; what the start would gain with no wait for the tables; which part of the gated products holds up stretch 3, DVE's steps, the reads or SP's queue; and what the 20.7 us are that remain without the gated products. The round of a score tile through maximum, exponential and two buffers would fit the waits at the scores, and was not tried by itself.
